# MLP activations transposed by DMA in 16-bit halves instead of on TensorE, in a hybrid attention and MLP layer on one core

## The chip, the cores and the metric

The kernel runs on one core of one Trainium2 chip. The metric is the device time of one execution in microseconds (us). The kernel before took 1346.14 us, the median of three runs (1346.04 to 1346.71).

## What is computed

One layer of a diffusion backbone over two groups of 128 tokens with 2048 features: context tokens (`x_prompt`) and latent tokens (`x_sample`). Both use the same weights, in float32. Cut to what matters:

```python
def sq_relu_mlp(h, w_up, w_down):
    return jnp.square(jax.nn.relu(h @ w_up)) @ w_down

# for each group x, with its own modulation vectors from ada_mod(c, w_ada, b_ada)
h = rms_norm(x, norm1_w) * (1 + sc1) + sh1
qa, ka, va, qb, kb, vb, ga, gb = project_heads(h, w_in, ...)   # 2048 x 8704
oa, ob = attention A (8 heads, 2 key heads), attention B (8 heads)
x = x + g1 * ((sigmoid(ga) * (oa @ w_br_a) + sigmoid(gb) * (ob @ w_br_b)) @ w_out)
h2 = rms_norm(x, norm2_w) * (1 + sc2) + sh2
x = x + g2 * sq_relu_mlp(h2, w_up, w_down)                     # 2048 -> 8192 -> 2048
```

The change lies between `h @ w_up` and `@ w_down`: the squared activations must have their hidden features on the partitions before they can be the stationary operand of the second product.

## The kernel before

Each weight tile is 128 x 1024 float32 (512 KB, two blocks of 128 rows by 512 columns). A tile is one **step** of the list `wsteps`. SP loads it (`raw`, in `add_step`); ScalarE copies it to a rounded high part (`wH`, `prep_hi`); VectorE subtracts to get the low part (`wL`, `prep`). A product of two float32 operands is then three matmuls of 512 columns: high by high, high by low, low by high (`mm3`, L284 to L286). A plain step has 12 matmuls: two blocks, two token groups, three parts.

Nothing is scheduled by a tool. `run` walks the steps in order and records for each of them, on every engine's in-order queue: the loads that are due (`RUN` says for each step how many steps ahead), the splits up to `LOOK` steps ahead, the step's matmuls, and then the functions that `at(i, fn)` put on step `i`. All the tables of numbers at the top are such places. All large buffers (4 KB a partition) come from one pool of `GEN` = 48. A load waits until its buffer is free, and SP's later transfers wait behind it.

The stages follow each other: modulation and the input projection (`w_in`, attention beside it), the branch products (`w_br_a`, `w_br_b`) with the gates, `w_out`, then the MLP. Gates named in `AWAY` are written to device memory and come back `GATE_BACK` steps before they are used. Steps in `LO_DMA` and `XL_DMA` get their low part from ScalarE and an accumulating transfer in POOL's queue instead of VectorE. `DOTS`, `DOTS1` and `DOTS2` place dot products of the modulation on VectorE.

The MLP's hidden width has 16 **units** of 512 columns, in eight pairs (`PIECES`). Pair 0 is done plainly (`up_unit`). Each other pair p is `up_pair(p)`, 16 steps in eight groups of two. A group in `FAST[p]` uses a scheme with seven block products instead of eight (21 matmuls instead of 24), for which VectorE and ScalarE form sums of the weight blocks (`prep_x`, `prep_y`: `t`, `tH`, `tL`, `uH`, `uL`, `XH`, `XL`, `YB`). There are 37 such groups. After a pair the activations are `up` tiles, tokens on the partitions. `up_T` transposes them with `tT` (L792 to L800): per unit eight TensorE transposes of 128 x 128 into PSUM (`ps_T`, L797), two ScalarE copies to the high half `aH` and two VectorE subtractions to `aL`. `T_PAIR` says at which step. Then `down_unit(p, n)` multiplies with `w_down`, four units of four steps, after each pair's successor has been computed; the partial sums are added by VectorE, or by an accumulating transfer in POOL's queue where `SUM_DMA` says so.

Of the kernel before, what the change touches and what calls it, by code (L numbers as in the profile page):

```python
# [10 lines left out]
F32 = mybir.dt.float32  # L11
F32R = mybir.dt.float32r
BF16 = mybir.dt.bfloat16
AF = mybir.ActivationFunctionType
OP = mybir.AluOpType
AX = mybir.AxisListType

P = 128
# [10 lines left out]
PIECES = [[2 * i, 2 * i + 1] for i in range(8)]  # L29
# [2 lines left out]
FB_DVE = 6  # L32
FB1 = 14
H_AT = 41
DOTS1 = [6, 8, 15, 20, 28, 30, 31, 38]
CHUNKS = [2, 2, 2, 4, 6]
NFAST = 8
FAST = {1: (0, 1, 5, 6, 7), 2: (0, 3, 4, 6, 7), 3: (0, 2, 4, 5, 7), 4: (0, 2, 3, 5, 7), 5: (0, 1, 2, 4, 5, 7), 6: (0, 2, 4, 6, 7), 7: (0, 1, 2, 4, 5, 7)}
SUM_DMA = [5, 6, 9, 10, 11, 12, 13, 15, 16, 19, 20, 21, 23, 25, 27]
AWAY = [('gA', 1), ('gB', 0), ('gA', 2)]  # L40
GATE_BACK = 3
DIRECT = (3,)
LO_DMA = [70, 83, 86, 107, 131, 176, 184, 186, 196, 233, 242, 292, 314, 328, 357, 379, 402, 435]
LO_AHEAD = 2

LOOK = "523112344222344433223333332123333453344534332454455544344533333544324554444555556665556644444333333333332222122213444544555434333333342344333334333323445565533344456656533344434444445455564546555554444443322355444554433333333434334433333333333654654332334455554444555653323314333422222223443233333332223323365455454443222212233432443334434743443332222333423323333333333325434322223333433323333334555543365365433333332222554442122132334343222223332233345544"
RUN = "454562331000011222223333322222222222222233345555544455434445554445665555555664543433234334444445665543321222222212444444444444442222222232223344444455544544444444443344343334466644455555554543255444343355556866544443566553333323333345552332222222223445332333333333332211122222332233322211233323323332333223333333332343322211333343333322233333444433643333312222334443322333233322222222322333443434455544333120222222232111233456655566567556322325335553333333"
CONST_AT = [60, 65]
XL_DMA = [40]
ADA_AT = [None, 4, 13, 21, 21, 34, 30]  # L50
XS_AT = {1: 13, 2: 18, 3: 29}
POST = {('kvA', 0): [67, 69, 71], ('qA', 0): [70, 73, 75], ('qA', 1): [74, 76, 82], ('kB', 0): [78, 84, 89], ('qB', 0): [82, 84, 93], ('kB', 1): [85, 90, 93], ('qB', 1): [91, 94, 96]}
JOBS = [[78, 79, 81, 83, 94], [82, 83, 87, 90, 94], [88, 89, 91, 93, 98], [93, 93, 95, 98, 102], [96, 97, 100, 105, 112], [102, 103, 107, 112, 120], [105, 107, 111, 118, 120], [112, 114, 117, 120, 122]]
SS_AT = [48, 56, 66, 75, 139, 139]
T_AT = [4, 4]
PREP_IN = [6, 7]
DOTS = [32, 39, 41, 43, 47, 47, 48, 49, 51, 52, 53, 55, 60, 64, 67, 69, 72, 76, 76, 83, 89, 90, 92, 92, 94, 98, 101, 103, 103, 105, 108, 111, 111, 112, 115, 118, 120, 122, 123, 123, 124, 128, 129, 129, 131, 132, 133, 137, 137, 137, 138, 143, 144, 147, 147, 150, 153, 157, 158, 160, 165, 167, 168, 168, 170, 172, 175, 177, 177, 178, 179, 183]
DOTS2 = [232, 233, 235, 237, 240, 242, 262, 265, 269, 270, 272, 289, 297, 299, 302, 306, 307, 326, 327, 332, 334, 335, 358, 361, 364, 365, 368, 370, 393, 394, 397, 401]
STAT_AT = [-1, -1, 10, 12]
T_PAIR = [[11, 11], [7, 15], [13, 13], [16, 16], [9, 9], [12, 12], [12, 12]]  # L60
COL = {"qA": 0, "kvA": 1024, "qB": 1536, "kB": 2560, "vB": 3584, "gA": 4608, "gB": 6656}


# [1 line left out]
def tile_hybrid_step(ctx: ExitStack, tc: tile.TileContext, a):  # L65
# [10 lines left out]
    def G(name, dt=F32):  # L76
        return gp.tile([P, 1024], dt, name=name, tag="g")
# [7 lines left out]
    def copy(out, in_):  # L85
        act.activation(out, in_, AF.Copy)  # L86
# [102 lines left out]
    def at(i, fn):  # L189
        cal.setdefault(i, []).append(fn)  # L190
# [361 lines left out]
    def end_of(key):  # L552
        return max(st["i"] for st in wsteps if st["key"] == key)
# [238 lines left out]
    def tT(src, hi, lo):  # L792

        for s in range(2):
            ps = bank("ps_T")
            for k in range(4):
                pe.transpose(ps[:, k * P:(k + 1) * P], src[:, s, k * P:(k + 1) * P], ident)  # L797
            psv = ps.rearrange("p (k t) -> p k t", k=4)
            copy(hi[:, :, s, :], psv)
            dve.tensor_tensor(lo[:, :, s, :], psv, hi[:, :, s, :].bitcast(F32), op=OP.subtract)  # L800

    def HL(name):
        return [G(name + x, F32R).rearrange("p (k s t) -> p k s t", k=4, s=2) for x in "HL"]
# [254 lines left out]
    def up_pair(p):  # L1058
# [32 lines left out]
        for pos, is_fast in enumerate(kinds):  # L1091
# [50 lines left out]
            def mm_y(st, b=b, j=j, pos=pos, end=end):  # L1142
                u0, u1 = (G(f"up{n}").rearrange("p (s n) -> p s n", s=2) for n in (n0, n1)) if end else (None, None)
                if end:
                    copy(u0[:, 0, :], box["Q1"])
                lo, hi = slice(0, 512), slice(512, 1024)
                todo = [("Q6", sc(j, 1), b["uH"][:, lo], b["uL"][:, lo]), ("Q2", x(j, 1, 0), b["YB"][:, lo], b["YB"][:, hi]),
                        ("Q7", sc(j, 2), b["tH"][:, hi], b["tL"][:, hi]), ("Q4", x(j, 1, 1), b["uH"][:, hi], b["uL"][:, hi]),
                        ("Q5", sc(j, 0), b["tH"][:, lo], b["tL"][:, lo])]
                if end or pos == 0:  # L1150
                    todo.append(("Q3", sc(j, 3), b["XH"][:, hi], b["XL"][:, hi]))
                if not end:
                    todo = [todo[i] for i in ((1, 2, 0, 4, 5, 3) if pos == 0 else (1, 4, 2, 3, 0))]
# [295 lines left out]
```

## Time and profile before

| | |
|---|---|
| median of three runs | 1346.14 us |
| the profiled execution's own time | 1346.98 us |
| its span (first to last instruction) | 1344.9 us |
| TensorE (PE) busy | 1331.6 us, 99% |
| VectorE (DVE) busy | 1194.9 us, 89% |
| ScalarE (ACT) busy | 738.8 us, 55% |
| GpSimd (POOL) busy | 66.7 us, 5% |
| DMA | 385.44 MB, mean 287 GB/s |

The profile is of one execution. PEld is the load of the stationary operand, which overlaps the matmuls. A record of a matmul is longer than the distance to the next one, because matmuls are pipelined; the distance is what a matmul costs. In a row of a group, `out<-in` names the tiles, `x128` is the count, then come busy us, mean ns of one, and the idle time just before them with what ended it. The chain that ended last is followed back from the last instruction, at each step to what released it.

### The profile page before, as it was taken

What the parts mean: (1) busy time and instruction counts of PE and PEld (TensorE: products, weight loads), DVE (VectorE), ACT (ScalarE), POOL (GpSimd) and SP (SyncE); (2) the same over time, 40 slices, a digit from 0 to 9 for tenths busy, and PEclk for the clock granted to TensorE, in tenths of its full rate; (3) what the DMA queues carried; (4) which work ended last, traced back from release to release, by engine and by line L of the source; (5) the groups of instructions that cost most, each with busy time, mean ns of one, the idle gap of its engine ahead of it and who ended that gap; (6) DMA issues with size and microseconds to landing.
All of it is one profiled execution on the core that took longest, in us unless ns stands there. A gap on an engine that the chain in (4) does not pass through costs nothing.

```text
span 1344.9 us, 18331 instructions
## 1 busy us (share of the span) xinstructions
PE 1331.6 (99%) x6552; PEld 1081.6 (80%) x6552; DVE 1194.9 (89%) x1568; ACT 738.8 (55%) x966; POOL 66.7 (5%) x76
## 2 busy tenths in 40 slices
PE   8899999999999999999999999999999999999998
PEld 4577788888788878888888888888888888888887
DVE  4689999988898999998789999998999999899675
ACT  5524443566656544345666665565665656556540
POOL 0000001332000000000000000000000000000000
PEclk9899999999999999999999999999999999999999
DMA  9999998977688999798466666888798887769942
GB/s 370 410 409 408 404 366 352 375 215 271 193 282 299 377 397 344 284 332 290 175 232 230 240 219 245 271 264 279 231 317 239 265 285 216 267 191 302 373 151 93
DMA packets 109611, 385.44 MB, mean 287 GB/s; under 512 B 12368, under 2 KB 13584, under 8 KB 109520
## 3 DMA queue, kind: packets, MB, share of 16 engines
q1 hardware_dynamic: 104064, 365.05, 73.5%
q0 software_dynamic: 5312, 19.14, 7.5%
q8 instruction: 51, 0.84, 0.3%
q14 instruction: 40, 0.33, 0.1%
q10 hardware_dynamic: 144, 0.08, 0.0%
HBM read 369.25 MB, written 7.11 MB: 280 GB/s over the span
## 4 chain that ended last, share of the span: by engine, by line
PE 96%; DMA 3%; DVE 1%; issue 0%; ACT 0%; SPq 0%; DVEq 0%
PE acc L284 17%; PE acc L286 17%; PE acc L285 17%; PE Q L1068 6%; PE Q L1070 6%; PE Q L1069 6%; PE acc L384 4%; PE acc L386 4%; PE acc L385 4%; PE ps_ada L301 2%; DMA raw<-in_w_in 2%; PE ps_T L797 1%; PE ps_S L700 1%; DMA araw<-in_w_pair 1%; PE Z L1070 1%; PE Z L1069 1%
## 5 line engine op out<-in xcount | busy, mean ns | idle before, releaser
L234 DVE TENSOR_TENSOR wL<-raw,wH 128x1024 fp32r<-128x1024 f32 x361 | 430.7, 1225 | 79.6 <-ACT wH L86 72.6
L86 ACT ACTIVATE wH<-raw 128x1024 fp32r<-128x1024 f32 (+1 forms) x385 | 385.6, 1047 | 138.6 <-PE acc L285 33.0
L384 PE MATMUL acc<-wH,hH 128*128 128x512 f32 x276 | 109.9, 398 | 0.0
L386 PE MATMUL acc<-wH,hL 128*128 128x512 f32 x276 | 108.4, 393 | 0.7 <-DVE hL L90 0.7
L385 PE MATMUL acc<-wL,hH 128*128 128x512 f32 x276 | 108.5, 393 | 0.0
L284 PE MATMUL acc<-wH,hH 128*128 128x512 f32 x256 | 101.8, 398 | 0.0
L286 PE MATMUL acc<-wH,hL 128*128 128x512 f32 x256 | 99.8, 390 | 0.0
L285 PE MATMUL acc<-wL,hH 128*128 128x512 f32 x256 | 99.7, 389 | 0.0
L1278 DVE CUSTOM_DVE_ANT_0 aT<-aT,cB,cols 128x1024 f32<-128x1024 f32 x56 | 71.5, 1284 | 0.2
L1278 DVE CUSTOM_DVE_ANT_0 junk<-aT,cB,cols 128x1024 bf16<-128x1024 f32 x56 | 71.3, 1279 | 0.0
L86 ACT ACTIVATE tH<-t 128x1024 fp32r<-128x1024 f32 x37 | 39.3, 1062 | 56.9 <-DVE t L1123 42.0
L384 PEld LDWEIGHTS acc<-wH,hH 128*128 128x128 f32 x276 | 52.3, 190 | 14.2 <-issue 3.3
L386 PEld LDWEIGHTS acc<-wH,hL 128*128 128x128 f32 x276 | 52.4, 190 | 12.3 <-DVE hL L90 1.1
L385 PEld LDWEIGHTS acc<-wL,hH 128*128 128x128 f32 x276 | 52.4, 190 | 10.5
L86 ACT ACTIVATE uH<-raw 128x1024 fp32r<-128x1024 f32 x37 | 39.3, 1063 | 36.2 <-DVE raw L1128 35.2
L286 PEld LDWEIGHTS acc<-wH,hL 128*128 128x128 f32 x256 | 48.1, 188 | 10.3
L285 PEld LDWEIGHTS acc<-wL,hH 128*128 128x128 f32 x256 | 48.1, 188 | 9.6 <-issue 0.2
L284 PEld LDWEIGHTS acc<-wH,hH 128*128 128x128 f32 x256 | 48.1, 188 | 9.6 <-issue 0.2
L1123 DVE TENSOR_TENSOR t<-raw 128x1024 f32<-128x1024 f32 x37 | 45.1, 1220 | 5.8 <-PE Z L1069 1.9
L1176 ACT ACTIVATE up<-up 128x1024 f32<-128x1024 f32 x28 | 29.7, 1062 | 33.0 <-DVE up L1170 32.6
L86 ACT ACTIVATE dsum<-acc 128x512 f32<-128x512 f32 x38 | 22.0, 595 | 45.2 <-PE acc L286 42.1
L1133 DVE TENSOR_TENSOR uL<-raw,uH 128x1024 fp32r<-128x1024 f32 x37 | 45.1, 1219 | 0.1
(629 smaller groups left out, 3320.4 us busy)
## 6 DMA issues: line engine op xcount, KB each, us to landing
raw<-in_w_in SPq DMA_DIRECT2D x133, 512.0 KB, 6.7
raw<-in_w_down SPq DMA_DIRECT2D x128, 512.0 KB, 5.9
araw<-in_w_pair SPq DMA_DIRECT2D x80, 512.0 KB, 9.6
raw<-in_w_upF SPq DMA_DIRECT2D x74, 512.0 KB, 5.2
aT<-in_w_gT SPq DMA_DIRECT2D x64, 512.0 KB, 6.6
raw<-in_w_up SPq DMA_DIRECT2D x54, 512.0 KB, 5.1
aT<-in_w_adaT SPq DMA_DIRECT2D x48, 512.0 KB, 7.4
raw<-in_w_out SPq DMA_DIRECT2D x32, 512.0 KB, 9.5
```

The costliest lines, as they stand in the source:

```text
L86: act.activation(out, in_, AF.Copy)
L234: dve.tensor_tensor(st["lo"], st["raw"], st["hi"].bitcast(F32), op=OP.subtract)
L284: pe.matmul(acc[tb], sh, wh[:, k, :], start=f, stop=False)
L285: pe.matmul(acc[tb], sh, wl[:, k, :], start=False, stop=False)
L286: pe.matmul(acc[tb], sl, wh[:, k, :], start=False, stop=l)
L384: pe.matmul(acc[tb], sh, wh[:, k, :], start=kt == 0 and k == 0, stop=False)
L385: pe.matmul(acc[tb], sh, wl[:, k, :], start=False, stop=False)
L386: pe.matmul(acc[tb], sl, wh[:, k, :], start=False, stop=last and k == 1)
L1068: pe.matmul(acc, stat[0], hi, start=f, stop=False)
L1069: pe.matmul(acc, stat[0], lo, start=False, stop=False)
L1070: pe.matmul(acc, stat[1], hi, start=False, stop=l)
L1278: dve.tensor_tensor_reduce(out, box["raw"], cB[s, tag], 1.0, dst if second else baT[:, part, fb:fb + 1], OP.mult, OP.add, dst)
```

## The change

The eight TensorE transposes of a unit are replaced. ScalarE copies the low and the high 16 bits of each word into two planes (`up_planes`); one transposing transfer in SP's queue, which also carries the weights, turns the planes around, 16 blocks of 128 x 128 halfwords (`up_flip`); ScalarE puts the halves together again, and the split into `aH` and `aL` works from SBUF (`up_T`). The three places are set by `P_UP`, `P_PAIR` (planes), `FLIP` (transfer, one step later) and `T_UP`, `T_PAIR` (merge and split). Unit 1, which was transposed within pair 1, is now placed like the others. The groups of seven products become 34 instead of 37; six instead of three gates go away and come back; the other tables have new numbers.

```diff
-DOTS1 = [6, 8, 15, 20, 28, 30, 31, 38]
+DOTS1 = [6, 8, 13, 20, 28, 30, 30, 37]
-FAST = {1: (0, 1, 5, 6, 7), 2: (0, 3, 4, 6, 7), 3: (0, 2, 4, 5, 7), 4: (0, 2, 3, 5, 7), 5: (0, 1, 2, 4, 5, 7), 6: (0, 2, 4, 6, 7), 7: (0, 1, 2, 4, 5, 7)}
-SUM_DMA = [5, 6, 9, 10, 11, 12, 13, 15, 16, 19, 20, 21, 23, 25, 27]
-AWAY = [('gA', 1), ('gB', 0), ('gA', 2)]
-GATE_BACK = 3
+FAST = {1: (0, 6, 7), 2: (0, 2, 6, 7), 3: (0, 2, 4, 5, 7), 4: (0, 3, 4, 5, 7), 5: (0, 1, 2, 3, 6, 7), 6: (0, 2, 4, 5, 7), 7: (0, 1, 2, 4, 5, 7)}
+SUM_DMA = [5, 6, 10, 11, 13, 15, 16, 19, 21, 23, 25, 26, 27]
+AWAY = [('gA', 1), ('gB', 0), ('gA', 2), ('gB', 3), ('gA', 0), ('gB', 2)]
+GATE_BACK = 4
-LO_DMA = [70, 83, 86, 107, 131, 176, 184, 186, 196, 233, 242, 292, 314, 328, 357, 379, 402, 435]
+LO_DMA = [70, 83, 107, 131, 176, 184, 186, 233, 292, 314, 328, 379, 402, 404, 435]
-XL_DMA = [40]
+XL_DMA = [28, 40, 42, 53]
-T_PAIR = [[11, 11], [7, 15], [13, 13], [16, 16], [9, 9], [12, 12], [12, 12]]
+T_PAIR = [[9, 9], [6, 8], [8, 9], [7, 9], [7, 11], [8, 9], [8, 11]]
+P_PAIR = [[3, 4], [2, 4], [3, 4], [1, 3], [2, 6], [3, 4], [3, 6]]
+FLIP = 1
+P_UP = [0, 2]
+T_UP = [9, 7]
...
+    def halves(name):
+        return gp.tile([P, 2048], U16, name=name, tag="g")
+    planes = {}
+    def up_planes(n):
+        src = up_r.pop(n).rearrange("p s (k f) -> p k s f", k=4).bitcast(U16).rearrange("p k s (f h) -> p h k s f", h=2)
+        pl = planes[n] = halves(f"pl{n}")
+        dst = pl.rearrange("p (h k s f) -> p h k s f", h=2, k=4, s=2)
+        for h in range(2):
+            copy(dst[:, h], src[:, h])
+    def up_flip(n):
+        pl, planes[n] = planes[n], halves(f"plT{n}")
+        sync.dma_start_transpose(planes[n].rearrange("p (j t) -> p j t", t=P), pl)
     def up_T(n):
         aH[n], aL[n] = HL(f"a{n}")
-        tT(up_r.pop(n), aH[n], aL[n])
+        full = G(f"aF{n}")
+        copy(full.bitcast(U16).rearrange("p (c h) -> p h c", h=2), planes.pop(n).rearrange("p (h c) -> p h c", h=2))
+        split(aH[n].rearrange("p k s t -> p (k s t)"), aL[n].rearrange("p k s t -> p (k s t)"), full)
...
-        if n != PIECES[0][1]:
-            at(end_of(("up", n)) + 2, lambda: up_T(n))
+        at(end_of(("up", n)) + P_UP[n], lambda: up_planes(n))
+        at(end_of(("up", n)) + P_UP[n] + FLIP, lambda: up_flip(n))
+        at(end_of(("up", n)) + T_UP[n], lambda: up_T(n))
...
-                    if p == 1:
-                        up_T(PIECES[0][1])
...
-            for n, i in zip(PIECES[p + 1], T_PAIR[p]):
-                at(len(wsteps) + i, lambda n=n: up_T(n))
+            for n, i, j in zip(PIECES[p + 1], P_PAIR[p], T_PAIR[p]):
+                at(len(wsteps) + i, lambda n=n: up_planes(n))
+                at(len(wsteps) + i + FLIP, lambda n=n: up_flip(n))
+                at(len(wsteps) + j, lambda n=n: up_T(n))
```

`LOOK`, `RUN`, `CONST_AT`, `ADA_AT`, `POST`, `JOBS`, `SS_AT`, `PREP_IN`, `DOTS`, `DOTS2` and `STAT_AT` change too, mostly by a few steps in a part of their entries; they are left out here.

More of the change, by code (lines that the diff above doesn't have):

```diff
@@ L13 @@
 BF16 = mybir.dt.bfloat16
+U16 = mybir.dt.uint16
 AF = mybir.ActivationFunctionType
@@ L42 @@
+SUM_DMA = [5, 6, 10, 11, 13, 15, 16, 19, 21, 23, 25, 26, 27]
+AWAY = [('gA', 1), ('gB', 0), ('gA', 2), ('gB', 3), ('gA', 0), ('gB', 2)]
+GATE_BACK = 4
 DIRECT = (3,)
-LO_DMA = [70, 83, 86, 107, 131, 176, 184, 186, 196, 233, 242, 292, 314, 328, 357, 379, 402, 435]
+LO_DMA = [70, 83, 107, 131, 176, 184, 186, 233, 292, 314, 328, 379, 402, 404, 435]
 LO_AHEAD = 2
-LOOK = "523112344222344433223333332123333453344534332454455544344533333544324554444555556665556644444333333333332222122213444544555434333333342344333334333323445565533344456656533344434444445455564546555554444443322355444554433333333434334433333333333654654332334455554444555653323314333422222223443233333332223323365455454443222212233432443334434743443332222333423323333333333325434322223333433323333334555543365365433333332222554442122132334343222223332233345544"
@@ L47 @@
-RUN = "454562331000011222223333322222222222222233345555544455434445554445665555555664543433234334444445665543321222222212444444444444442222222232223344444455544544444444443344343334466644455555554543255444343355556866544443566553333323333345552332222222223445332333333333332211122222332233322211233323323332333223333333332343322211333343333322233333444433643333312222334443322333233322222222322333443434455544333120222222232111233456655566567556322325335553333333"
-CONST_AT = [60, 65]
-XL_DMA = [40]
@@ L50 @@
-ADA_AT = [None, 4, 13, 21, 21, 34, 30]
+LOOK = "411111234222344433223333332123333453344534332454455544344534333544324554444555556665556644444333333333332222122212344544555434333333342344333334333323445566643344456656533344434444445455564546555554444554322355444554433333333434334433333333333654544332334455554444555653323314333422222223443233333332223323365455455443222212233432443334434753443333333444534434333333333325434322223333433333333334555643355353332222221111443442122132334453222223332233345544"
@@ new lines @@
+RUN = "662110000000000222223333322222222222222233345555544455434445554334554445555664543433234334444445665543321222222212444444444444442222222232223344444455544544444444443344343334466644455555554543255444343355445756544443566664333312222234552332222222223445332333333333332211122222332233322211233323323332332112344444442343322211333343333322233334544433743333312223445554422333233322222222322333333434456545333120222222232111233456655566567556322325335553333334"
+CONST_AT = [63, 64]
+XL_DMA = [28, 40, 42, 53]
@@ L51 @@
+ADA_AT = [None, 4, 13, 21, 21, 35, 30]
 XS_AT = {1: 13, 2: 18, 3: 29}
-POST = {('kvA', 0): [67, 69, 71], ('qA', 0): [70, 73, 75], ('qA', 1): [74, 76, 82], ('kB', 0): [78, 84, 89], ('qB', 0): [82, 84, 93], ('kB', 1): [85, 90, 93], ('qB', 1): [91, 94, 96]}
-JOBS = [[78, 79, 81, 83, 94], [82, 83, 87, 90, 94], [88, 89, 91, 93, 98], [93, 93, 95, 98, 102], [96, 97, 100, 105, 112], [102, 103, 107, 112, 120], [105, 107, 111, 118, 120], [112, 114, 117, 120, 122]]
-SS_AT = [48, 56, 66, 75, 139, 139]
+POST = {('kvA', 0): [67, 70, 73], ('qA', 0): [70, 74, 76], ('qA', 1): [72, 74, 80], ('kB', 0): [79, 85, 92], ('qB', 0): [82, 84, 93], ('kB', 1): [85, 90, 93], ('qB', 1): [90, 93, 96]}
@@ L55 @@
+JOBS = [[79, 80, 80, 84, 93], [82, 83, 87, 90, 94], [88, 89, 91, 93, 98], [93, 93, 95, 98, 102], [96, 97, 100, 105, 112], [102, 103, 107, 112, 123], [105, 107, 111, 118, 121], [112, 115, 118, 121, 123]]
+SS_AT = [47, 57, 69, 75, 139, 139]
 T_AT = [4, 4]
-PREP_IN = [6, 7]
-DOTS = [32, 39, 41, 43, 47, 47, 48, 49, 51, 52, 53, 55, 60, 64, 67, 69, 72, 76, 76, 83, 89, 90, 92, 92, 94, 98, 101, 103, 103, 105, 108, 111, 111, 112, 115, 118, 120, 122, 123, 123, 124, 128, 129, 129, 131, 132, 133, 137, 137, 137, 138, 143, 144, 147, 147, 150, 153, 157, 158, 160, 165, 167, 168, 168, 170, 172, 175, 177, 177, 178, 179, 183]
@@ L58 @@
-DOTS2 = [232, 233, 235, 237, 240, 242, 262, 265, 269, 270, 272, 289, 297, 299, 302, 306, 307, 326, 327, 332, 334, 335, 358, 361, 364, 365, 368, 370, 393, 394, 397, 401]
-STAT_AT = [-1, -1, 10, 12]
-T_PAIR = [[11, 11], [7, 15], [13, 13], [16, 16], [9, 9], [12, 12], [12, 12]]
+PREP_IN = [6, 5]
+DOTS = [32, 39, 42, 43, 47, 47, 49, 50, 52, 54, 55, 57, 59, 62, 69, 70, 73, 77, 79, 85, 90, 91, 92, 92, 94, 98, 101, 103, 103, 105, 108, 111, 111, 112, 115, 118, 120, 122, 122, 123, 126, 127, 128, 130, 130, 132, 134, 137, 137, 138, 138, 143, 144, 147, 147, 150, 153, 155, 156, 160, 164, 167, 170, 170, 172, 174, 177, 178, 178, 178, 179, 182]
@@ L61 @@
+DOTS2 = [233, 235, 236, 237, 240, 243, 258, 263, 265, 269, 270, 271, 289, 297, 300, 301, 306, 307, 328, 328, 333, 334, 335, 358, 360, 361, 363, 366, 367, 390, 395, 399]
+STAT_AT = [-1, -1, 10, 13]
+T_PAIR = [[9, 9], [6, 8], [8, 9], [7, 9], [7, 11], [8, 9], [8, 11]]
[3 more added lines that the diff above has]
+T_UP = [9, 7]
 COL = {"qA": 0, "kvA": 1024, "qB": 1536, "kB": 2560, "vB": 3584, "gA": 4608, "gB": 6656}
```

## The prediction

> **What bounds the kernel now.** First the page's busy times, then busy time by stage, then the chain that ended last.
>
> ```profile
> PE 1331.6 (99%) x6552; PEld 1081.6 (80%) x6552; DVE 1194.9 (89%) x1568; ACT 738.8 (55%) x966; POOL 66.7 (5%) x76
> PE 96%; DMA 3%; DVE 1%; issue 0%; ACT 0%; SPq 0%; DVEq 0%
> ```
>
> TensorE is busy 99% of the span, and the chain that ended last runs through it for 96%. Busy time alone can hide pipelining, so the stages and the cadence follow (columns of the first fence: stretch, its length, then busy us and count for PE, PEld, DVE, ACT, POOL, the granted clock, the DMA share, GB/s).
>
> ```profile
> 0.00:60.00 60.00, 51.47 (x308) 29.14 (x308) 28.73 (x53) 33.40 (x56) 2.00 (x10) 0.94 1.00 388
> 480.00:580.00 100.00, 100.00 (x506) 82.20 (x499) 98.50 (x135) 44.70 (x50) 0.86 (x1) 1.00 0.91 336
> 720.00:1260.00 540.00, 540.00 (x2432) 448.09 (x2431) 506.90 (x590) 332.55 (x377) 19.04 (x22) 1.00 0.79 260
> 1260.00:1345.00 85.00, 80.17 (x362) 66.28 (x361) 55.18 (x68) 29.21 (x34) 2.58 (x3) 0.99 0.52 170
> ```
>
> ```profile
> 704.99 0.39 PE L1068 MATMUL Q<-XH,sH 128*128 128x512 f32 x1
> ...
> 725.16 0.39 PE L1070 MATMUL Z<-wH,h23L 128*128 128x512 f32 x1
> ```
>
> The second fence is the timeline. There are 89 products between those two starts, so one 512-column product costs 20.17 / 89 = 0.2266 us of TensorE; its 0.39 us record is pipeline depth. From 720 to 1260 us, the heart of the MLP, TensorE has no idle time at a full clock. VectorE follows at 506.9 of 540 (94%), ScalarE at 62%, and the DMA engines show a share of 0.79. The idle time (13.3 us of 1344.9) lies in the first 60 us and at the end. So a product or a transpose taken out of TensorE in the MLP shortens the run by its cadence, as long as no other engine takes its place.
>
> **Transposes that go.** The chain in order of time shows them:
>
> ```profile
> 681.58 0.87 PE ps_T L797 x8
> 772.47 1.75 PE ps_T L797 x16
> ...
> 1286.73 1.75 PE ps_T L797 x16
> ```
>
> ```profile
> L797 PE MATMUL ps_T<-ident,up 128*128 128x128 f32 x128 | 15.6, 272 | 0.0
> ```
>
> Eight transposes take 0.87 us of the chain, 0.109 us each. There are 128 on `up` tiles (16 units of 8), hence 128 x 0.109 = 14.0 us. The busy time of that group, 15.6 us, is the upper bound, since it overlaps the neighbouring product. All 128 lie on the path: nothing else was running on TensorE meanwhile. The order of the changed program has none of them left (404 operations of 128 columns become 276).
>
> **Groups of seven products.** FAST goes from 37 entries to 34. A group of seven issues 21 matmuls, a plain one 24, so 3 x 3 = 9 products come back: 9 x 0.2266 = +2.0 us. The changed order has 5,399 instead of 5,390 matmuls of 512 columns, which is those 9. TensorE's net is -14.0 + 2.0 = **-12.0 us**.
>
> **VectorE and ScalarE.** Rows for the prices:
>
> ```profile
> L234 DVE TENSOR_TENSOR wL<-raw,wH 128x1024 fp32r<-128x1024 f32 x361 | 430.7, 1225 | 79.6 <-ACT wH L86 72.6 <-issue 2.6 <-PE ps_PT L746 2.6
> L1131 DVE TENSOR_TENSOR XL<-raw,XH 128x1024 fp32r<-128x1024 f32 x36 | 43.9, 1219 | 0.3 <-DMA dsum<-dsum 0.3
> L1126 DVE TENSOR_TENSOR raw<-t,raw 128x512 f32<-128x512 f32 x37 | 25.6, 692 | 1.3
> L1210 DVE TENSOR_TENSOR dsum<-dsum,acc 128x512 f32<-128x512 f32 x18 | 11.8, 683 | 3.4 <-PE acc L286 3.4
> L86 ACT ACTIVATE wH<-raw 128x1024 fp32r<-128x1024 f32 x379 | 382.1, 1054 | 138.6 <-PE acc L285 33.0 <-PE acc L385 22.0 <-PE acc L286 9.9
> L86 ACT ACTIVATE dsum<-acc 128x512 f32<-128x512 f32 x38 | 22.0, 595 | 45.2 <-PE acc L286 42.1 <-PE acc L285 2.1
> ```
>
> ```profile
> 682.05 1.09 ACT L86 ACTIVATE a0H<-ps_T 128x512 fp32r<-128x512 f32 x2
> 683.65 1.28 DVE L800 TENSOR_TENSOR a0L<-ps_T,a0H 128x512 fp32r<-128x512 f32 x2
> ```
>
> VectorE: three groups lose t, tL and uL (all of XL's shape, 1.22 us) and three half-width steps of 0.69 us: -3 x 5.73 = -17.2. XL is made there 30 instead of 36 times: -7.3. The wL splits grow by 9 (6 plain steps, 3 fewer entries in LO_DMA): +11.0. Two entries fewer in SUM_DMA put 4 adds back: +2.7. The low halves become 16 x 1.22 instead of 32 x 0.64: -1.0. The sum is -11.8 us, about what TensorE loses, so VectorE stays just behind it and becomes no bound.
>
> ScalarE: 32 copies of 1024 halfwords into planes, 33.7 us if a halfword costs what a word costs in the wH row; 16 merging copies of 2048 halfwords, 33.7; 16 high halves, 16.9, for 32 of 0.545, -17.4. The groups give back 3 x (3 x 1.05 + 0.6) = 11.3, six plain splits add 6.3, SUM_DMA -2.4. Sum about +60 us. No row here has 16-bit operands: the copies could take half that, or double (+127 us in all). From 720 to 1260 us ScalarE's 332.6 of 540 us rise to about 72% (83% at the upper price), still below VectorE. I take +60 and charge nothing: ScalarE's copies run a few steps ahead of the products that use them, and what VectorE waits for wH now (72.6 us, in the wL row) has left TensorE without idle time there. POOL gets three more XL transfers and five fewer of wL and dsum: no cost.
>
> **The transposing transfer.** Each unit now sends 512 KB from SBUF to SBUF through SP's queue. No transposing transfer is in this trace. Nearest rows (size, median us from issue to landing):
>
> ```profile
> raw<-in_w_down SPq DMA_DIRECT2D x128, 512.0 KB, 5.9
> raw<-in_w_upF SPq DMA_DIRECT2D x74, 512.0 KB, 5.2
> gm_gB<-g_gB SPq DMA_DIRECT2D x1, 512.0 KB, 2.6
> out_y_sample<-x1b SPq DMA_DIRECT2D x2, 128.0 KB, 1.9
> wb<-in_q_norm_a SPq DMA_DIRECT2D x1, 64.0 KB, 4.5
> ```
>
> The low end is 2.6 us, 512 KB leaving SBUF. The high end is 8 x 4.5 = 36 us, if 512 KB moved in short rows scaled with the 64 KB load of 512-byte rows, which is mostly latency. I take 5.5 us, what the same bytes take in the same queue and stage. What does that touch? SP waits in order for ScalarE's planes, and the weight loads recorded behind wait with it; ScalarE waits in order at the merging copy, and the wH splits behind it wait. P_PAIR, FLIP and T_PAIR put the merge 3 to 8 steps behind the transfer; a step of 12 products is 2.72 us, so 8.2 to 21.8 us. In the changed order, the first load behind a transfer feeds TensorE at the tightest 73 products (16.6 us) after the product that releases the transfer's chain, at the median about 106 (24 us). From that go two plane copies (2.1), the load's landing (5.2), wH (1.05) and wL (1.22), in all 9.6 us. So a transfer may hold the queue 7 us at the tightest place, 14 at the median, 28 at the widest, before TensorE waits. At 5.5 us all sixteen are covered; cost 0. Bandwidth: 16 x 512 KB between 680 and 1290 us is 14 GB/s beside 260, while the first stage moves 388.
>
> Against this stands a rule of the Trainium skill, page "VectorE: DVE Perf Modes", section "The three transpose paths": a 128x128 block of 16-bit data takes 1309 ns by DMA and 390 ns on TensorE, and it advises TensorE where the result may go to PSUM. This trace has 0.109 us a block on TensorE where the page has 0.390, so the measurement decides and the page's figures look like those of one operation alone. Sixteen blocks at 1309 ns would be an estimated 20.9 us a transfer (rival 2). The page "Advanced Engine Details and Errata" of the Trainium skill, section "X-Bar Transpose (TRN2)", says the opposite, that transposing DMAs are as fast as plain ones; no run here shows either yet.
>
> **The rest of the tables.** AWAY sends three more gates out and back: 3.1 MB, 8 us of DMA time at 388 GB/s, within some 190 us of share about 0.9 (window 480 to 580) where TensorE has no idle time. I take 0, with 8 us as the bound. The shifted dots, loads and lookaheads move nothing off TensorE; the first 60 us hold 8.5 us of idle time, from which they can gain or lose a little: 0, within 3.
>
> **Sum.** The profiled execution took 1346.98 us (span 1344.9 and 2.1 around it), 0.84 more than the median 1346.14. 1346.98 - 12.0 = 1335.0, against the median **1334.2 us**.
>
> **Rivals.**
> 1. *The queue is held longer than the cover.* With the sixteen allowances (7, 9.6, 9.8, four near 12.5, four near 15.2, 18, 20, 24, 26, 28 us), a hold of 12.5 us makes three places wait 5.5 + 2.9 + 2.7 = 11 us: the gain is gone, and that is where it decides. At 15 us the waits are about 28, net +16: 1362 us. For it: loads and transfer share one in-order queue. Against it: 12.5 is twice the row of the same bytes.
> 2. *The blocks are served one after another.* Sixteen at the 1.9 us of the smallest output rows is 30 us; over the allowances that is 16 x 30.4 - 253 = 233 us, so about 1567 us. Against it: the 512 KB that leave SBUF take 2.6 us, not four times the 1.9 of 128 KB. By the estimate of 20.9 us from "VectorE: DVE Perf Modes" of the Trainium skill it would be 97 us of waits and about 1431 us.
> 3. *Short waits eat part.* The planes and their transposed copy hold two more of the 48 buffers, so some loads start late. SP already waits mostly for buffers:
>
> ```profile
> SPq L208 <- PE acc L286: 257.6, 80, 9.3
> ```
>
> A third to two thirds of 12 us lost gives 1338 to 1342.
> 4. *The time goes to another bound*, VectorE at 94%, or DMA around the gates (8 us): with 8 to 12 us lost, 1342 to 1346.
>
> **Chances.** The forecast 0.58; rival 3 0.15 (still faster); rival 4 0.05, of which 0.04 counts as no change; rival 1 0.17 and rival 2 0.05, both slower. Within 0.2% (2.7 us, about what a measurement of this kernel can tell) is no change: faster 0.74, same 0.04, slower 0.22. The range begins at 1330 (busy-time bound of the transposes, 1.6 us, and 3 us at the start) and ends at 1352, in the lower part of rival 1, so that about 0.2 lies above it. The likeliest case alone spans 1331 to 1338.
>
> **What would show it.** Right: no `ps_T<-ident,up` rows; TensorE busy near 1319 us with the 720 to 1260 stretch still without idle time; VectorE near 1183 and ScalarE near 800; the transposing transfer landing within 7 us. Wrong: idle TensorE in stretches of several us after the pairs, put down to wH or raw; a landing over 12 us; ScalarE idle at the merging copy for a DMA.

## The result, and the profile after

The changed kernel takes 1348.28 us (median of 20 runs, 1345.22 to 1358.25) beside 1346.39 us for the kernel before (20 runs on the same chip, 1344.5 to 1347.52): a ratio of 1.0023, interval 1.0013 to 1.0034. It is slower by 2 to 3 us; the forecast was 12 us faster. The profiled execution took 1348.4 us with a span of 1346.6.

The page of the changed kernel, busy times and the chain that ended last:

```profile
PE 1323.7 (98%) x6433; PEld 1071.3 (80%) x6433; DVE 1183.2 (88%) x1541; ACT 799.7 (59%) x988; POOL 65.9 (5%) x74
PE 90%; DMA 4%; DVE 3%; issue 2%; ACT 1%; SPq 0%; DVEq 0%; ACTq 0%; POOLq 0%
```

TensorE's busy time fell by 7.9 us (1331.6 to 1323.7), but its idle time rose from 13.3 to 22.9 us, by 9.6. The sum, +1.7, is the change of the span. The chain now leaves TensorE for VectorE and DMA. Where, the busy time by stretch shows (length, then busy us and count of PE, PEld, DVE, ACT, POOL, the granted clock, the DMA share, GB/s):

```profile
0.00:60.00 60.00, 51.13 (x310) 28.89 (x311) 28.27 (x52) 33.18 (x55) 2.00 (x10) 0.97 0.98 387
480.00:580.00 100.00, 100.00 (x494) 82.40 (x487) 97.85 (x134) 46.34 (x52) 0.85 (x1) 1.00 0.93 353
720.00:1260.00 540.00, 530.75 (x2318) 436.65 (x2317) 499.95 (x573) 378.31 (x392) 18.14 (x21) 0.99 0.85 267
1030.00:1040.00 10.00, 8.35 (x32) 6.18 (x31) 9.85 (x12) 6.76 (x9) 0.85 (x1) 0.89 0.95 326
1210.00:1220.00 10.00, 5.61 (x16) 4.47 (x17) 9.86 (x12) 6.16 (x8) 0.86 (x1) 0.66 0.73 210
```

The start and the gate stage are as before. Nearly all of the new idle time, 9.25 us, lies between 720 and 1260 us, where TensorE had none. The last two rows are its worst places, at the starts of pair 5 and pair 7. In both VectorE is busy 9.85 of 10 us although its mean over the stage fell to 500 of 540. At the same place the kernel before looked like this:

```profile
1030.00:1040.00 10.00, 10.00 (x46) 8.29 (x45) 9.84 (x12) 5.85 (x8) 0.00 (x0) 1.00 0.68 259
```

VectorE was full there already, and TensorE just didn't wait for it. A full stretch alone is no wait: in the kernel before, VectorE was busy 9.8 us or more in 30 of the 54 stretches of 10 us between 720 and 1260. Now TensorE's list of waits has these (engine, tile, line, releaser; us in total, times, longest):

```profile
PE Q L1096 <- ACT dsum L91: 7.4, 3, 5.6
PE Q L1097 <- DMA XL<-in_w_upF: 1.1, 1, 1.1
```

The list names ScalarE's copy of `dsum`, which empties a PSUM bank. The timeline of ScalarE at the start of pair 7 shows that this copy isn't the cause:

```profile
1194.64 2.52 ACT L91 ACTIVATE aF<-plT 128x2048 uint16<-128x2048 uint16 x1 [3.69 <-DMA plT<-pl]
...
1210.80 1.06 ACT L91 ACTIVATE tH<-t 128x1024 fp32r<-128x1024 f32 x1 [2.02 <-DVE t L1151]
1212.80 1.06 ACT L91 ACTIVATE uH<-raw 128x1024 fp32r<-128x1024 f32 x1 [0.94 <-DVE raw L1156]
1213.76 1.07 ACT L91 ACTIVATE dsum<-acc 128x512 f32<-128x512 f32 x2
```

The bracket is the engine's idle time and what ended it. `dsum` stands in ScalarE's in-order queue behind `tH` and `uH` of the pair's second group of seven. Those wait for `t` and `raw` from VectorE, which works through the groups without a gap. The waits that end on ScalarE are VectorE's lateness, passed on. VectorE comes late to pair 7. Just before, it stood still: from 1190 to 1200 us it is busy 3.22 of 10 us, and its own row says what it waited for, the merged activations:

```profile
1190.00:1200.00 10.00, 9.67 (x43) 8.02 (x44) 3.22 (x5) 6.27 (x6) 0.00 (x0) 1.00 0.93 257
1198.28 1.23 DVE L95 TENSOR_TENSOR a13L<-aF,a13H 128x1024 fp32r<-128x1024 f32 x1 [6.24 <-ACT a13H L91]
```

The chain in order of time (start us, us, what) leads from a transposing transfer of 13.02 us through ScalarE's merge and VectorE's preparation to TensorE:

```profile
1181.60 13.02 DMA plT<-pl
...
1194.64 2.53 ACT aF L91
...
1197.19 1.07 ACT a13H L91
...
1202.97 1.15 DVE t L1151
...
1212.07 0.70 DVE raw L1156
...
1213.76 0.59 ACT dsum L91
1214.39 0.80 PE Q L1096
...
1216.04 0.43 PE Q L1096
...
1218.17 0.43 PE Q L1098
...
1218.95 0.23 PE Q L1097
```

After the wait of 5.6 us TensorE issues a product every 0.43 us for 4 us, then every 0.23 again; the stretch of 1210 to 1220 shows a granted clock of 0.66. The wait of 1.5 us at pair 5 is followed by such products too. So these waits cost more than their length: seven slow products at pair 5 and eight at pair 7 add some 3 us, most of the reason why TensorE's busy time fell by 7.9 us and not by 12.

What one group of seven costs VectorE, from the groups by shape (count, busy us, mean ns, then idle time ahead of them):

```profile
L1151 DVE TENSOR_TENSOR t<-raw 128x1024 f32<-128x1024 f32 x34 | 41.5, 1220 | 5.7 <-PE Q L1097 2.8 <-PE Z L1097 1.7 <-DMA raw<-in_w_upF 1.1
L1154 DVE TENSOR_TENSOR raw<-t,raw 128x512 f32<-128x512 f32 x34 | 23.5, 692 | 1.2
L1159 DVE TENSOR_TENSOR XL<-raw,XH 128x1024 fp32r<-128x1024 f32 x30 | 36.6, 1219 | 0.0
L1160 DVE TENSOR_TENSOR tL<-t,tH 128x1024 fp32r<-128x1024 f32 x34 | 41.4, 1218 | 0.0
```

Four steps of 1.22 us (`t`, `tL`, `uL`, `XL`) and three of 0.69 make 6.95 us, but the records overlap a little. From one group's `t` to the next, with no idle time between, it is 6.60 us (the starts below, from VectorE's timeline at pair 7):

```profile
1202.89 1.22 DVE L1151 TENSOR_TENSOR t<-raw 128x1024 f32<-128x1024 f32 x1
...
1209.49 1.22 DVE L1151 TENSOR_TENSOR t<-raw 128x1024 f32<-128x1024 f32 x1
...
1216.09 1.22 DVE L1151 TENSOR_TENSOR t<-raw 128x1024 f32<-128x1024 f32 x1
```

TensorE needs 21 products of 0.2266 for it, 4.76 us. A plain group costs VectorE two `wL` splits, 2.28 us from start to start (1199.42 to 1201.70), and TensorE 24 products, 5.44. A group of seven and a plain one in turn are 8.88 against 10.20 us, and VectorE keeps up as far as this work goes; three groups of seven in a row put it 5.5 us behind, four 7.4. Pair 5 of the changed kernel begins with four in a row, (0, 1, 2, 3), pair 7 with three.

### The profile page after: what moved, and what is told of

Its sections match the earlier page's. It is cut to its first block, busy times and chain, and to the rows that moved or that the text cites. A ratio compares the mean times of both kernels' runs of the same rounds, so it can differ in the third digit from the quotient of the medians.

```text
span 1346.6 us, 18148 instructions
## 1 busy us (share of the span) xinstructions
PE 1323.7 (98%) x6433; PEld 1071.3 (80%) x6433; DVE 1183.2 (88%) x1541; ACT 799.7 (59%) x988; POOL 65.9 (5%) x74
## 2 busy tenths in 40 slices
DMA packets 143466, 395.91 MB, mean 294 GB/s; under 512 B 45712, under 2 KB 46928, under 8 KB 143376
## 4 chain that ended last, share of the span: by engine, by line
PE 90%; DMA 4%; DVE 3%; issue 2%; ACT 1%; SPq 0%; DVEq 0%; ACTq 0%; POOLq 0%
PE acc L289 16%; PE acc L290 16%; PE acc L291 16%; PE Q L1096 6%; PE Q L1097 6%; PE Q L1098 6%; PE acc L389 5%; PE acc L391 4%; PE acc L390 4%; PE ps_ada L306 2%; DMA araw<-in_w_pair 2%; DMA plT<-pl 1%; PE ps_S L705 1%; PE Z L1096 1%; PE Z L1097 1%
## 5 line engine op out<-in xcount | busy, mean ns | idle before, releaser
L239 DVE TENSOR_TENSOR wL<-raw,wH 128x1024 fp32r<-128x1024 f32 x370 | 439.9, 1225 | 74.4 <-ACT wH L91 72.2
L91 ACT ACTIVATE wH<-raw 128x1024 fp32r<-128x1024 f32 (+1 forms) x391 | 390.7, 1045 | 121.8 <-PE acc L390 19.3
L91 ACT ACTIVATE tH<-t 128x1024 fp32r<-128x1024 f32 x34 | 36.1, 1061 | 50.3 <-DVE t L1151 46.7
L91 ACT ACTIVATE uH<-raw 128x1024 fp32r<-128x1024 f32 x34 | 36.1, 1062 | 32.6 <-DVE raw L1156 26.9
L1151 DVE TENSOR_TENSOR t<-raw 128x1024 f32<-128x1024 f32 x34 | 41.5, 1220 | 5.7 <-PE Q L1097 2.8
L306 PE MATMUL ps_ada<-araw,cpad 128*32 128x256 f32 x640 | 39.8, 384 | 4.8 <-DMA araw<-in_w_pair 4.6
L91 ACT ACTIVATE aF<-plT 128x2048 uint16<-128x2048 uint16 x16 | 40.5, 2533 | 6.6 <-DMA plT<-pl 5.6
```

The costliest lines, as they stand in the source:

```text
L239: dve.tensor_tensor(st["lo"], st["raw"], st["hi"].bitcast(F32), op=OP.subtract)
```

## The experiments

Every ratio is to the kernel before on the same chip (medians 1344.9 to 1345.5 us there). Edits are to the changed kernel unless said otherwise. The expectations name theories by letters. A: a late transposing transfer holds ScalarE at the merge. B: ScalarE's added copies do. C: the new tables cost the time. D: the transfers' packets slow the loads. E: VectorE has no time to spare at the starts of the pairs. F: POOL's low parts of `XL` come late. G: POOL's adds make the transposing transfer late. H: groups of seven in a row run at VectorE's pace.

**Which part costs: transposing or tables.** TensorE's transposes with the new tables, and the transposing transfer with the old ones (all tables of the diff but `P_PAIR`, `FLIP`, `P_UP`, `T_UP` and `T_PAIR`):

```diff
-        copy(full.bitcast(U16)..., planes.pop(n)...)
-        split(aH[n]..., aL[n]..., full)
+        tT(up_r.pop(n), aH[n], aL[n])
```

> The changed kernel with all its new tables, but with the MLP activations transposed on TensorE again, at the places of the new T_PAIR; planes, transposing transfers and merging copies are left out. Theory A (a transposing transfer that lands late holds ScalarE at the merging copy, and the PSUM banks that ScalarE has to empty come free late), theory B (the added ScalarE copies alone are enough for that) and theory D (the transfers' packets slow the loads): no such stalls, so TensorE's count decides: 1346.4 + 2.0 for nine more products = 1348.4 us. Theory C (the new tables with 34 groups cost the time): the stalls stay, about 1360 us.

Measured: 1355.15 us, 1.0075 (1.0063 to 1.0087), some 8 us more than the 9 products account for, and between the two expected times. TensorE waits in a place that was without idle time:

```profile
PE Q L1094 <- DMA XL<-in_w_upF: 4.0, 1, 4.0
```

```diff
-FAST = {1: (0, 6, 7), 2: (0, 2, 6, 7), ..., 7: (0, 1, 2, 4, 5, 7)}
-XL_DMA = [28, 40, 42, 53]
+FAST = {1: (0, 1, 5, 6, 7), 2: (0, 3, 4, 6, 7), ..., 7: (0, 1, 2, 4, 5, 7)}
+XL_DMA = [40]
...
```

> The new way of transposing (planes, transfers, merging copies at the new places) with all other tables of the kernel before: 37 groups of seven, its SUM_DMA, LO_DMA, LOOK, RUN and so on. TensorE has 14.0 us less than before. C (the new tables cost the time): 1332 to 1336 us. E: VectorE keeps the load that it had before while TensorE's time shrinks, so the stalls are as large as in the changed kernel or larger: 1346 to 1358 us.

Measured: 1359.35 us, 1.0108 (1.0093 to 1.0122), idle time of 0.5 us or more in ten places of the MLP. So the new tables alone lose and the new transposing alone loses; the tables fit the transposing in part. With the new tables, taking TensorE's transposes out is worth 1.0075 - 1.0023 = 0.0052, 7 us of the 14.

**The transfer.** Left out, and sent without anyone waiting for it:

```diff
     def up_flip(n):
-        pl, planes[n] = planes[n], halves(f"plT{n}")
-        sync.dma_start_transpose(planes[n]..., pl)
+        pass
```

> The changed kernel without the transposing transfers: the merging copy reads the planes directly, so the activations are left untransposed; all ScalarE copies stay. A and D: the stalls go, 1334 to 1337 us. B and C: they stay, 1346 to 1350 us.

Measured: 1343.39 us (1339.96 to 1347.26), 0.9988 (0.9975 to 1.0), between the two expected times. In the profiled execution, a slower one of 1346.83 us, waits stay without any transfer, though the one at pair 7 falls from 5.6 to 2.3 us:

```profile
PE Q L1096 <- DMA XL<-in_w_upF: 4.3, 1, 4.3
PE Q L1095 <- ACT dsum L91: 4.2, 3, 2.3
```

```diff
-        sync.dma_start_transpose(planes[n]..., pl)
+        sync.dma_start_transpose(halves(f"plT{n}")..., planes[n])
```

> The changed kernel with the transposing transfers issued at the same places, but into a buffer that nobody reads: the merging copy reads the planes directly (activations untransposed), so ScalarE never waits for a transfer while the queue and the DMA engines carry it. A: 1334 to 1338 us. D: 1346 to 1350, since the queue's load is unchanged. B and C: 1346 to 1350.

Measured: 1347.09 us, 1.0011 (0.9999 to 1.0023). Sixteen transfers in the queue (with the buffers that they fill) cost some 3 us (1.0011 - 0.9988), being waited for some 1.5 more; the intervals overlap, so the split is rough. At 4.7 us in all the transfer is the smaller part.

**More time for the transfer.**

```diff
-T_PAIR = [[9, 9], [6, 8], [8, 9], [7, 9], [7, 11], [8, 9], [8, 11]]
+T_PAIR = [[12, 12], [9, 11], [11, 12], [10, 12], [10, 14], [11, 12], [11, 14]]
```

> The changed kernel with every T_PAIR three steps (8 us) later, so that a late transfer has landed before ScalarE comes to the merging copy. A: most of the loss returns, 1335 to 1340 us. B, C and D: nothing changes, 1346 to 1350 us.

Measured: 1368.74 us, 1.0175 (1.0162 to 1.0189), far above both expected times. The merge was moved away from the transfer and towards the next pair, and the pair's start became the worse for it:

```profile
PE Q L1096 <- ACT dsum L91: 19.0, 4, 8.0
```

At the wait of 8.0 us the chain shows how: the `t` of one of pair 7's groups stands right behind `a13L` in VectorE's order, and `a13L` waits for the merge.

**Less work on VectorE, elsewhere.**

```diff
     def dot(...):
+        if which == "g2" and second: return
```

> The changed kernel without the second half of the dot products for gate 2 (32 VectorE operations of 1.28 us and their 32 reads of the sum, 44 us, all between the steps 306 and 399; gate 2 is then only half summed). Theory E (at the starts of pairs 4, 5 and 7 VectorE has no time to spare; ScalarE's preparation of the pair's second group waits for VectorE's sums, and the dsum copies that empty the PSUM banks stand behind it in ScalarE's order): the stalls at pairs 4 and 5 go, 1338 to 1342 us. Theory F (the low parts that POOL's accumulating transfers make for the new XL_DMA entries arrive late): 1345 to 1349. Theory A (late transposing transfers): 1345 to 1349.

Measured: 1346.9 us, 1.0013 (1.0003 to 1.0024); 38 us less work on VectorE moved nothing, and E's forecast fails. Two rows show why:

```profile
1030.00:1040.00 10.00, 8.53 (x37) 6.40 (x36) 9.86 (x13) 6.63 (x8) 1.72 (x2) 1.00 1.07 332
DVE a8L L95 <- ACT a8H L91: 7.0, 1, 7.0
```

At the start of pair 5 VectorE is as full as with the dots. It can't use the time that they leave: just ahead, at 1014 us, it now stands still for 7.0 us (0.5 in the changed kernel) until ScalarE has merged the activations. At pair 7 the wait for `dsum` falls from 5.6 to 2.3 us, while waits for POOL's `XL` rise from 1.1 to 4.4 us in all (the profiled execution took 1344.57 us).

**The bank copies, and POOL's transfers of XL.** Fewer steps of lookahead ahead of the bank copies; XL made on VectorE again; both:

```diff
-LOOK at steps 310, 311, 342, 343, 406, 407: 5, 5, 4, 4, 5, 3
+LOOK at steps 310, 311, 342, 343, 406, 407: 3, 2, 3, 2, 3, 2
```

> The changed kernel with six entries of LOOK lowered (steps 310, 311, 342, 343, 406, 407), so that ScalarE comes to the last dsum copies of a piece before it prepares the second group of the next pair; no work is added or left out. E: the three bank stalls shrink, 1338 to 1342 us. A and F: 1345 to 1349.

Measured: 1346.58 us, 1.0013 (1.0 to 1.0025). The waits for `dsum` are gone and others stand in their place:

```profile
PE Q L1097 <- DMA XL<-in_w_upF: 5.4, 1, 5.4
PE Q L1097 <- DVE XL L1159: 2.1, 3, 1.5
```

```diff
-XL_DMA = [28, 40, 42, 53]
+XL_DMA = [40]
```

> The changed kernel with XL_DMA back to [40]: three low parts on VectorE (3.7 us) instead of POOL's queue. F: 1343 to 1345 us. E and A: 1347 to 1350.

Measured: 1345.03 us, 0.9994 (0.9985 to 1.0003); the waits for `dsum` are 7.7 us.

> The changed kernel with the six lowered LOOK entries and XL_DMA back to [40], both edits together. If bank stalls and late XL transfers only take each other's place (one hides the other), both have to go for a gain: 1337 to 1341 us. If neither carries the loss, 1344 to 1348.

Measured: 1344.25 us, 0.9989 (0.998 to 0.9998). With both edits the waits end on VectorE itself:

```profile
PE Q L1097 <- DVE XL L1159: 6.8, 5, 2.3
```

**POOL's accumulating transfers beside the slow transposing one.**

```diff
-LO_DMA = [..., 379, 402, 404, 435]
+LO_DMA = [..., 379, 435]
```

> The changed kernel without the LO_DMA entries 402 and 404, whose accumulating transfers run in POOL's queue beside the transposing transfers of units 12 and 13; VectorE makes these two low parts (2.4 us). Theory G (accumulating transfers beside a transposing one make it late, 13 us instead of 5): the slowest transfer lands within 8 us, ScalarE's wait for it and the 5.6 us bank stall at pair 7 go, 1340 to 1344 us. Otherwise: the slowest transfer stays over 11 us, 1347 to 1350.

Measured: 1344.86 us, 1.0001 (0.9992 to 1.0009). The slowest transfer still takes 13.0 us, so these two aren't its cause, and G falls; but ScalarE waits 1.5 us for the transfers instead of 5.6, and the time is 3 us better. Together with the two edits above:

> The three edits together: lowered LOOK entries, XL_DMA [40], no LO_DMA 402 and 404. If bank stalls, late XL and the late transfer are all that is lost: 1335 to 1338 us, TensorE idle below 15 us in all. If a further bound stands behind them: 1340 to 1346.

Measured: 1342.84 us, 0.998 (0.9972 to 0.9989); `DVE XL` still holds TensorE for 5.0 us. The three edits are worth 6 us and leave groups in a row as they are.

**Fewer groups in a row.** On top of the three edits:

```diff
-FAST = {..., 5: (0, 1, 2, 3, 6, 7), 6: (0, 2, 4, 5, 7), 7: (0, 1, 2, 4, 5, 7)}
+FAST = {..., 5: (0, 2, 4, 5, 7), 6: (0, 2, 4, 5, 7), 7: (0, 2, 4, 5, 7)}
```

> The three edits, and pairs 5 and 7 get the five spread groups of pair 3 instead of six with three or four in a row at the start (31 groups; 9 more products, TensorE +2.0 us; VectorE about 14 us less). Theory H (a group of seven takes VectorE 6.95 us and TensorE 4.8 us, so that groups in a row at a pair's start run at VectorE's pace): the stalls in pairs 5 and 7 go, 1335 to 1339 us and below the three edits alone. Otherwise 2 us above the three edits alone.

(The edit leaves 32 groups, not 31, and adds 6 products, 1.4 us.) Measured: **1335.26 us** (1333.37 to 1336.27), 0.9926 (0.9913 to 0.9938), though TensorE has more products. Its waits in the MLP are gone:

```profile
720.00:1260.00 540.00, 540.00 (x2380) 445.78 (x2379) 504.45 (x576) 379.80 (x394) 14.72 (x17) 1.00 0.84 270
1030.00:1040.00 10.00, 10.00 (x44) 8.02 (x44) 7.86 (x10) 5.55 (x7) 0.86 (x1) 1.00 1.02 354
```

VectorE's share of the stage is higher than in the changed kernel (504 of 540 against 500), and TensorE doesn't wait once; at 1030 us it is 7.86 instead of 9.85 of 10. The spreading without the three edits, and in pair 5 alone:

> The changed kernel with only the groups of pairs 5 and 7 spread, (0, 2, 4, 5, 7) in both: 32 groups, TensorE +1.4 us for 6 more products, VectorE about 9 us less. Theory H (groups of seven in a row at a pair's start run at VectorE's pace) as the main cause: 1335 to 1339 us. If the other three edits are needed too: 1341 to 1346.

Measured: 1339.09 us, 0.9957 (0.9942 to 0.9973); 3.8 us of waits for POOL's XL remain in the profiled execution, one of 1342.15 us.

> The changed kernel with only pair 5 spread (33 groups). H: the waits between 1030 and 1060 us go, those at pair 7 stay, 1341 to 1345 us. If pair 5 with its four groups in a row is the whole cause: 1335 to 1339. Otherwise 1347 to 1350.

Measured: 1344.13 us, 0.9998 (0.9987 to 1.0009): pair 7 seems the larger half.

**Is it only the spreading?** The kernel before, with its transposes, pairs 5 and 7 spread in the same way (35 groups):

> The kernel before, transposes on TensorE, with pairs 5 and 7 spread in the same way (35 groups instead of 37). Its MLP has no waits that spreading could remove, so by H it only pays for 6 more products: about 1347 us, 1.4 more than the kernel before. If spreading helps by itself: below 1344.

Measured: 1346.41 us, 1.001 (1.0001 to 1.0019), its 6 products. The spreading by itself earns nothing; it lets the missing transposes count. From here to the 1335 us above it is 0.9926 - 1.001 = -0.0084, 11.3 us, with 9 more products (2.0): the transposes are worth some 13.3 us, against 14.0 in the forecast, if the other tables and the three edits by themselves make no difference to a kernel without waits.

**Number or place?** 34 groups, two of them moved to pairs 1 and 2, with the three edits:

```diff
+FAST = {1: (0, 2, 6, 7), 2: (0, 2, 4, 6, 7), 3: (0, 2, 4, 5, 7), 4: (0, 3, 4, 5, 7), 5: (0, 2, 4, 5, 7), 6: (0, 2, 4, 5, 7), 7: (0, 2, 4, 5, 7)}
```

> The three edits and the spread pairs 5 and 7, with one group more in pair 1, (0, 2, 6, 7), and one more in pair 2, (0, 2, 4, 6, 7): 34 groups as in the changed kernel. If only the place of the groups counts: 1.4 us less than with 32 groups, 1333 to 1335 us. If the number counts, waits return in pairs 1 and 2: 1337 to 1345.

Measured: 1344.3 us, 0.9996 (0.9988 to 1.0005). TensorE now waits in pair 1:

```profile
PE Q L1097 <- DVE XL L1159: 5.5, 2, 5.3
```

```profile
700.00:710.00 10.00, 5.40 (x24) 4.13 (x22) 7.54 (x11) 6.19 (x8) 0.00 (x0) 0.92 0.61 168
```

VectorE isn't full there. Its own row of waits says what it stood for, right before (until 701.2 us):

```profile
DVE a0L L95 <- ACT a0H L91: 8.3, 1, 8.3
```

The same wait is 2.3 us in the changed kernel. So this run doesn't decide between number and place: with the groups moved, what holds TensorE in pair 1 is a standstill of VectorE at the merged activations, passed on.

**A rival: VectorE stands still at the merged activations.** In the changed kernel VectorE waits 16.6 us in all for `aH` ahead of `aL` (1.2 before), 6.2 of it just ahead of pair 7. Its part was put two steps later, without the three edits and with them:

```diff
-        split(aH[n]..., aL[n]..., full)
+        copy(aH[n]..., full); fulls[n] = full
+    def up_L(n):
+        dve.tensor_tensor(aL[n]..., fulls.pop(n), aH[n]..., op=OP.subtract)
...
+                at(len(wsteps) + j + 2, lambda n=n: up_L(n))
```

> The changed kernel with the low halves of the activations (aL, on VectorE) recorded two steps (5.4 us) behind the high halves (aH, on ScalarE), so that VectorE doesn't stand still while ScalarE merges; no work is taken out. In the changed kernel VectorE waits 16.6 us in all for aH (6.2 of them in front of pair 7), where the kernel before waits 1.2. Hand-off theory (VectorE comes to the pairs with nothing in hand because it stands still at aL): the waits for aH fall below 4 us, most of TensorE's 9.6 us of extra idle time goes, 1338 to 1341 us, ratio 0.994 to 0.996. Pace theory (groups of seven in a row cost VectorE 6.95 us each against 4.76 on TensorE, whatever it has in hand): the waits for aH fall too, but TensorE still waits in pairs 5 and 7; 1344 to 1348 us, ratio 0.999 to 1.002.

Measured: 1350.59 us, 1.0041 (1.0026 to 1.0057). The waits for `aH` are gone, but VectorE's waits for `wH`, which ScalarE makes behind the merging copies in its queue, rose from 72.2 us, and one wait for a transfer itself is new (last two rows). TensorE waits more (first two):

```profile
PE Q L1103 <- ACT dsum L91: 8.8, 3, 5.0
PE Q L1104 <- DVE XL L1166: 2.2, 2, 1.5
DVE wL L239 <- ACT wH L91: 84.7, 40, 8.1
DVE a12L L1023 <- DMA plT<-pl: 2.4, 1, 2.4
```

Ahead of pair 7 VectorE still stands for 2.4 and 3.3 us, 5.7 instead of 6.2. The edit moved the standstill and didn't take it away.

> The same with the three edits to the tables (LOOK, XL_DMA and LO_DMA, measured at 0.998 with the groups in a row left as they are). Hand-off theory: the remaining 5.0 us of waits for XL on VectorE go and the time comes to that of the spread groups, less the 1.4 us of their six products: 1333 to 1336 us, ratio 0.991 to 0.993. Pace theory: it stays near 0.998, 1341 to 1344 us.

Measured: 1348.7 us, 1.0022 (1.0012 to 1.0031), against 0.998 without the move; `DVE XL` rose from 5.0 to 9.9 us. Of that, 5.6 us are one wait at pair 5, behind another standstill of VectorE, for an accumulating transfer of POOL:

```profile
DVE t L1158 <- DMA dsum<-dsum: 4.9, 1, 4.9
```

With the three edits alone the same wait of VectorE is 2.7 us, and TensorE's behind it 3.3. So neither run took the standstill away, and they don't refute the hand-off theory. The start of pair 7 in the runs above tells more (profiled executions, us):

| run | groups of pair 7 | VectorE waits for `a13H` | TensorE's longest wait behind it |
|---|---|---|---|
| changed kernel | 0, 1, 2, 4, 5, 7 | 6.2 | 5.6 |
| XL on VectorE | the same | 8.6 | 5.6 |
| half of the dots | the same | 3.7 | 2.3 |
| pair 5 alone spread | the same | 3.6 | 3.4 |
| transfer unread | the same | 3.3 | 4.1 |
| no transfer | the same | 2.8 | 2.3 |
| no adds beside | the same | 2.4 | 2.7 |
| both pairs spread | 0, 2, 4, 5, 7 | 3.7 | none |

With the groups in a row, TensorE's wait is by and large long where the standstill is long; with the groups spread, a standstill of 3.7 us costs nothing. By these rows it takes both at pair 7: VectorE comes late, and then has work that is slower than TensorE's. At pair 5 of the changed kernel it stood only 1.4 us ahead of four groups in a row, and TensorE waits 1.5. Not tried were merged activations that come early with the groups left in a row, a longer stretch of lookahead for the groups' own preparation, and why one transposing transfer in the sixteen is slow.

## Why the prediction was wrong, step by step

**Failed: "VectorE stays just behind it and becomes no bound".** The step compared totals (-11.8 against -12.0 us) and a stage's mean (94%). Both totals came true; what decides is the place. Where groups of seven stand close together, VectorE needs 6.60 us for what TensorE now does in 4.76, and after a delay it can't catch up. The time taken out of TensorE came back there as 9.6 us of idle time and some 4 us of slow products. Rival 4 named this bound at a chance of 0.05, and for that it said "1342 to 1346" with the gain lost; the gain was lost, and 2 us more. That closely placed groups cost most of the gain is shown by the runs that spread them: 9 us better without the three edits, 7 us with them, while the kernel before only pays for its products. The 6.60 against 4.76 us is arithmetic that agrees.

**Failed: "I take +60 and charge nothing" for ScalarE's copies.** The reason given was that VectorE's waits for `wH` had left TensorE without idle time. Those waits stayed (72.6 to 72.2 us), but the merge added a second kind: VectorE's waits for `aH` rose from 1.2 to 16.6 us, 6.2 of them just ahead of pair 7, where TensorE's longest wait follows. How the loss at pair 7 divides between this standstill and the groups behind it isn't shown.

**Failed: "POOL gets three more XL transfers and five fewer of wL and dsum: no cost".** The waits for `XL` by DMA (1.1 us here, 3.8 in the run with spread groups alone, 5.4 with the copies first) are these; XL on VectorE takes them away, and that edit is worth 3.9 us (1.0023 - 0.9994). With the new tables and TensorE's transposes they were the largest wait, 4.0 us.

**Partly wrong: the transfer's cover.** Forecast 5.5 us and all sixteen covered. The tile's own rows:

```profile
L1010 SPq DMA_TRANSPOSE plT<-pl x16: 1704/2803/8281, 679.4 to 1271.4; - x16
DMA to landing us min/median/max: 4.2/5.1/13.0
```

The median, 5.1 us, is a little below what the forecast took. The page "Advanced Engine Details and Errata" of the Trainium skill, section "X-Bar Transpose (TRN2)", says that transposing transfers are as fast as plain ones, and the median agrees: the plain weight loads of the same size take 5.4 and 6.0 us here. The estimate of 20.9 us from the page "VectorE: DVE Perf Modes" of the Trainium skill is not borne out: sixteen blocks in 5.1 us are 0.32 us a block. But the slowest took 13.0, over the tightest cover of 7 us, and the cover was reckoned through the weight loads only. ScalarE stood 3.69 us at the merge of that one, and VectorE's 6.2 us ahead of pair 7 follow from it. Rivals 1 and 3 looked for late loads behind the transfer, and none of TensorE's waits in the MLP ends on a weight load of that queue; the path that hurt runs through the merge. At 4.7 us in all (the run without the transfer) it alone would not have turned the sign. (In the list of allowances the median is near 15.2 us, where the text says 14; nothing hangs on it.)

**Right.** The transposes' 14.0 us (13.3 by the runs with spread groups). The products, 0.2266 us each. VectorE's total, -11.7 us for -11.8 forecast. ScalarE's, +60.9 for +60, with some luck: the plane copies took 1044 ns about as forecast, but the merging ones 2533 ns where 2.1 us was taken, 40.5 us instead of 33.7, and smaller terms that came out lower hid it.

```profile
L91 ACT ACTIVATE aF<-plT 128x2048 uint16<-128x2048 uint16 x16 | 40.5, 2533 | 6.6 <-DMA plT<-pl 5.6 <-PE acc L290 0.7 <-DMA dsum<-dsum 0.4
L91 ACT ACTIVATE pl<-up 128x1024 uint16<-128x1024 uint16 x32 | 31.9, 1044 | 1.4 <-PE acc L290 0.7 <-PE acc L291 0.6
```

The signs named in advance served: no TensorE transposes of `up` are left, and the stage with idle time and the landing over 12 us, both named as signs of error, are there, and so is ScalarE's idle time at the merging copy, 5.6 us for a transfer.

## What to carry to other kernels

When the bounding engine is relieved in a stage, compare the price of each repeated group on both engines (6.60 against 4.76 us here), not the next engine's share of the stage. A mean of 94% hid this; a full stretch of 10 us doesn't show it either, since the kernel before had many without a wait. Then look for what makes the next engine stand still ahead of such groups: here a step that waits in its in-order queue for a result that has come by way of a transfer and another engine. A wait on a bank copy or a transfer may be another engine's lateness passed through an in-order queue; follow the queue to the first instruction that had an idle bracket, and then ask what that engine stood for. Tables tuned around one bound should be moved with it: spreading the groups was worth nothing before the change and 7 to 9 us after.

## What the hardware showed

- A transposing transfer of 512 KB within SBUF landed in 4.2 to 13.0 us and held the issuing queue 1.7 to 8.3 us (median 2.8). In each of the sixteen kernels here that have these transfers, the slowest took between 10.8 and 15.5 us. The sixteen transfers show up as 33,280 more packets under 512 B (45,712 against 12,432 in the run that leaves only them out).
- ScalarE's 16-bit copies ran at the price of an element, not of a byte: 1.02 ns a halfword when gathered into planes, 1.24 ns when scattered back, against 1.03 ns for a word in the `wH` split.
- After a wait of 5.6 us TensorE issued products every 0.43 us instead of 0.227 for some 4 us, at a granted clock of 0.66 in that stretch. After a wait of 1.15 us at 1147.7 us there were no such products (clock 1.00).
